# Two-layer encoder trunk on one core: both ends of the program without GpSimd, and one of four low parts of the grouped heads on GpSimd

## The chip, the cores and the metric

The kernel runs on one core of one Trainium2 chip. The time is device time in microseconds (us) of one launch; the median of the runs counts. A core has TensorE (PE in the rows: matrix products and transposes, results into the accumulation memory PSUM), VectorE (DVE), ScalarE (ACT), GpSimd (POOL) and SyncE (SP, which issues the DMAs). They run side by side and wait for each other through semaphores.

## The reference, cut to what matters

Sixteen learned tokens are put ahead of 1024 tokens of width 1024. Two layers follow, each a mixer and a squared-ReLU MLP, and a last norm:

```
h = concat(meta, x)                                   # 1040 x 1024
for i in (0, 1):
    hn = rmsnorm(h, norm_attn[i])
    h = h + (even_mixer(hn) if i == 0 else odd_mixer(hn))
    h = h + relu(rmsnorm(h, norm_mlp[i]) @ w_up[i])**2 @ w_down[i]
return rmsnorm(h, norm_final)[:, 16:]
```

`even_mixer` projects once and feeds two kinds of heads: four differential heads (A), `softmax(q0 k0 + bias) - lam * softmax(q1 k1 + bias)`, and eight query heads in two groups that share keys and values (B, the grouped heads): rms-normed and rotated queries and keys, `softmax(q k) @ v`. `odd_mixer` is windowed attention. `rmsnorm(x, g) = x * rsqrt(mean(x*x) + eps) * g`.

## The kernel before

Everything lies transposed: features on the 128 partitions, the 1040 tokens along a row, in chunks of 348, 346 and 346. For precision each operand of a product is split in a high part `h` (a rounding copy) and a low part `l = x - h`, and a product is three matmuls: high by high, high by low, low by high (`mm3`, line 149). A program orders each engine's instructions ahead of time: among what its model takes to be ready it prefers what stands earlier in the code, and it gives a tile a buffer when one of its tag is free. On the chip each engine then runs its list strictly in that order.

**Opening** (lines 236 to 263). For each chunk and each of eight feature blocks k a DMA brings `hin`; the high part `hg0h` is made on VectorE for k in `HI_DVE` = 0, 2, 5 (line 245) and on ScalarE otherwise (line 247); the low part `hg0l` is made on VectorE (line 248). In the same pass the squares for the first norm are summed in two accumulators: GpSimd squares and adds blocks 0 to 2 (`SQ_POOL` = 3, lines 255 and 259), ScalarE squares the other five (line 257), VectorE adds them (line 259) and joins the two sums (line 260). `make_r` turns the sum into the row factor R: column sums on TensorE (`colsum`, line 192), an inverse root in some 13 tiny VectorE instructions (`rsqrt_small`, lines 157 to 163), a broadcast over the partitions on TensorE (`bcast_cols`, line 215) and a ScalarE copy out of PSUM (line 224). The first two projections (`early`, blocks 16 and 12) don't need R before they are evacuated.

**Grouped heads** (`attend_b`, line 691, 34 calls: 16 pairs of query tiles for each of two groups, and one call for the 16 tokens each). A call makes scores for two 128-row tiles (line 524), evacuates them with a running minimum on VectorE (line 529), takes exponentials on ScalarE (line 538) and scales by the inverse sum on GpSimd (line 700). Its second half, `pv` (line 545), comes three calls later (`AHEAD` = 3): the probabilities are transposed on TensorE in four runs of 512 columns (line 558); each run is copied to a high part `ph` on ScalarE (line 575), its low part `plo` is formed on VectorE (line 577), and TensorE multiplies both with the values (line 589). A last short piece (lines 599 to 602) handles 16 tokens. `pv` has a way for chosen runs (`lo_pool`): transposed first, copied raw on ScalarE, both parts formed on GpSimd in buffers of their own (`ph2`, `plo2`, one each), multiplied last. `LO_A` and `LO_B` are empty, so it isn't used. Probabilities of the A and B heads share one tag, `sp`, with `A_SP` = 11 buffers.

**End** (`dense(1, ...)`, last loop). The last products of the second MLP run for three groups of tokens (512, 256 and 256, `CH_LAST`). For each of eight blocks m: products (line 149), VectorE adds them to `hall` (line 1088), `finish1` squares on ScalarE (line 183), adds into `accf` (line 184; GpSimd in the first two groups, VectorE in the last) and scales by the gain on ScalarE (line 1313). Then `done1` makes the row factor in `accf` (through `make_r`) and multiplies the eight blocks with it (line 1318), on GpSimd in the first two groups; in the last, blocks 1 and 4 on GpSimd (`R_POOL`) and six on VectorE. Two blocks at a time go out by DMA (line 1322).

Of the kernel before, what the change touches and what calls it, by code (L numbers as in the profile page):

```python
# [12 lines left out]
F32 = mybir.dt.float32  # L13
F32R = mybir.dt.float32r
I32 = mybir.dt.int32
AF = mybir.ActivationFunctionType
ALU = mybir.AluOpType
# [4 lines left out]
P = 128  # L22
L = 1040
NM = 16
S = 1024
KT = 8
# [4 lines left out]
CH_ALL = ((0, 348), (348, 346), (694, 346))  # L31
# [12 lines left out]
OUT_K = 2  # L44
# [7 lines left out]
B_TAIL = 0, 0  # L52
CUT_K = ()
U3 = 1
R_DVE, R_POOL = (), (1, 4)
FAST0 = (0, 1)
POOL_K = 4
LO_A = ()
LO_B = ()
PH2 = 1  # L60
SQ_POOL = 3
HI_DVE = (0, 2, 5)
AHEAD = 3
A_SP = 11
AHEAD_C = 2
C_S, C_PH = 5, 3

# [1 line left out]
def f32(ap):  # L69
    return ap.bitcast(F32)  # L70


def trunk(tc, hT, gT, w_in0, w_out0, w_up, w_down, w_in1, w_out1, rel, sinks, lamv, subln, qkn,
          onehot, ident_d, cos_d, sin_d, out, dbg=None, stop=None):
    nc = tc.nc
    V, A, G, T, D = nc.vector, nc.scalar, nc.gpsimd, nc.tensor, nc.sync
# [3 lines left out]
    def nm(s):  # L80
        uid[0] += 1
        return f"{s}_{uid[0]}"

    def pool(name, side="left", bufs=1, **kw):
        return tc.alloc_tile_pool(name=name, bufs=bufs, side=side, reuse_waits="tile", **kw)

    def lay_out(pl, tags):

        kept = {}
        for tag, shape, dt, bufs in tags:  # L90
            kept[tag] = [pl.tile(shape, dt, tag=tag, bufs=bufs, name=nm(tag))]

        def get(tag, shape, dt, bufs):
            if kept.get(tag):
                return kept[tag].pop()
            return pl.tile(shape, dt, tag=tag, bufs=bufs, name=nm(tag))

        return get
# [4 lines left out]
    sm = pool("small", bufs=16)  # L103
    tp = pool("temps", bufs=3)
# [3 lines left out]
    def bank(ring):  # L108
        i = at.get(ring, 0)
        at[ring] = i + 1  # L110
        tag = RINGS[ring][i % len(RINGS[ring])]
        return psU.tile([P, 512], F32, tag=tag, bufs=BANKS[tag], name=nm(ring))
# [6 lines left out]
    gt = cst.tile([P, 5, KT], F32, name="gt")  # L119
# [50 lines left out]
    def tok_tiles(c0, n):  # L170
        return [(c0 + i * P, min(P, n - i * P)) for i in range((n + P - 1) // P)]
# [6 lines left out]
    def sq_acc(hk, acc, first, o, n, add_on=G):  # L178
        if first:
            A.activation(acc[:, o:o + n], hk[:, o:o + n], AF.Square)  # L180
        else:
            t = sqp[0].tile([P, 512], F32, tag="sq", bufs=1, name=nm("sq"))
            A.activation(t[:, :n], hk[:, o:o + n], AF.Square)
            add_on.tensor_tensor(acc[:, o:o + n], acc[:, o:o + n], t[:, :n], op=ALU.add)

    def colsum(acc, c0, n, ps, scale, eps=None, on=V):

        tiles = tok_tiles(c0, n)
        accs = acc if isinstance(acc, list) else [acc]
        for i, (o, w) in enumerate(tiles):  # L190
            for j, a in enumerate(accs):
                T.matmul(ps[:w, 2 * i:2 * i + 2], a[:, o:o + w], ones, start=(j == 0), stop=(j == len(accs) - 1))
        x = sm.tile([P, 24], F32, tag="cs", bufs=2, name=nm("cs"))
        nt = len(tiles)
        full = sum(1 for _, w in tiles if w == P)
        src = ps.rearrange("p (a b) -> p a b", b=2)
        if full < nt:
            V.memset(x[:, :nt], 1.0)
        if eps is None:
            V.tensor_scalar(x[:, :full], src[:, :full, 0], scale, EPS, op0=ALU.mult, op1=ALU.add)  # L200
        else:
            V.scalar_tensor_tensor(x[:, :full], src[:, :full, 0], scale, eps, op0=ALU.mult, op1=ALU.add)
        if full < nt:
            w = tiles[-1][1]
            V.tensor_scalar(x[:w, full:nt], src[:w, full:nt, 0], scale, EPS, op0=ALU.mult, op1=ALU.add)
        return rsqrt_small(x[:, :nt], P, nt, on), tiles

    def bcast_cols(y, tiles, newps, use):

        for b in range(0, len(tiles), 4):  # L210
            ps = newps()
            off = 0
            for i in range(b, min(b + 4, len(tiles))):
                w = tiles[i][1]
                T.matmul(ps[:, off:off + w], y[:w, i:i + 1].to_broadcast([w, P]), ident[:w, :w],  # L215
                         start=True, stop=True)
                off += w
            use(ps, tiles[b][0], off)

    def make_r(acc, c0, n, smps, newps):  # L220

        y, tiles = colsum(acc, c0, n, smps, 1.0 / 1024)
        r = acc
        bcast_cols(y, tiles, newps, lambda ps, o, w: A.copy(r[:, o:o + w], ps[:, :w]))
        return r
# [6 lines left out]
    getP = lay_out(pP, [("hl", [P, L], F32R, 4), ("zT", [P, L], F32, 2), ("vst", [P, NT, P], F32R, 2)])  # L232
    xh = [xp0.tile([P, L], F32R, tag="xh", name=f"hg0h{k}") for k in range(KT)]
    xl = [xp0.tile([P, L], F32R, tag="xl", name=f"hg0l{k}") for k in range(KT)]
    hin = [pR.tile([P, L], F32, tag="hin", bufs=8, name=f"hin{k}") for k in range(KT)]
    first_w = load_w(w_in0[16], parts=2)
    D.dma_start(gt, gT)
    sq0 = cst.tile([P, L], F32, tag="ra", name="sq0")
    sq = [sq0, f32(getP("hl", [P, L], F32R, 4))]
    for o, n in CH_ALL:  # L240
        c = slice(o, o + n)
        for k in range(KT):
            D.dma_start(hin[k][:, c], hT[k][:, c])
            if k in HI_DVE:
                V.tensor_scalar(xh[k][:, c], hin[k][:, c], gt[:, 0, k:k + 1], None, op0=ALU.mult)
            else:
                A.activation(xh[k][:, c], hin[k][:, c], AF.Copy, bias=0.0, scale=gt[:, 0, k:k + 1])
            V.scalar_tensor_tensor(xl[k][:, c], hin[k][:, c], gt[:, 0, k:k + 1], f32(xh[k][:, c]),
                                   op0=ALU.mult, op1=ALU.subtract)
            on_pool = k < SQ_POOL  # L250
            acc = sq[0] if on_pool else sq[1]
            first = k in (0, SQ_POOL)
            t = acc[:, c] if first else tp.tile([P, 520], F32, tag="t", name=nm("sq"))[:, :n]
            if on_pool:
                G.tensor_tensor(t, hin[k][:, c], hin[k][:, c], op=ALU.mult)
            else:
                A.activation(t, hin[k][:, c], AF.Square)
            if not first:
                (G if on_pool else V).tensor_tensor(acc[:, c], acc[:, c], t, op=ALU.add)
        V.tensor_tensor(sq0[:, c], sq0[:, c], sq[1][:, c], op=ALU.add)  # L260
    D.dma_start(ident, ident_d)
    R = make_r(sq0, 0, L, bank("nat"), lambda: bank("nat"))

# [157 lines left out]
    n = 260  # L421
    for o in range(0, 2080, n):
        ps = bank("nat")
        T.matmul(ps[:4, :n], relt[:, 0:4], oh[o // L][:, o % L:o % L + n], start=True, stop=True)
        t = tp.tile([P, 520], F32, tag="t", name=nm("bv"))[:, :512]
# [29 lines left out]
    for h in range(4):  # L455
# [9 lines left out]
        def put_tail(pt, b, n, w):  # L465
# [12 lines left out]
    pA = pool("att", side="left")  # L478
    getA = lay_out(pA, [("sp", [P, L], F32, A_SP), ("osq", [P, L], F32, 1), ("ph", [P, 512], F32R, 3),
                        ("plo", [P, 512], F32R, 3), ("oT", [P, L], F32, 2), ("ob", [64, 256], F32, 2),  # L480
# [123 lines left out]
    def prob():  # L604
        return getA("sp", [P, L], F32, A_SP)

# [84 lines left out]
    def attend_b(g, ptq, store):  # L691
# [10 lines left out]
        def values():  # L702
            po = bank("pv")
            yield from pv(po, ptiles, (vp[g],), ((0, 0), (0, 1)), LO_B)
            gw = sum(c for _, c, _ in ptiles)
# [33 lines left out]
    if stop == "mix0":  # L739
        tt = pool("dbgp", side="right", bufs=2)  # L740
        for k in range(8):
            m = tt.tile([P, L], F32, tag="m", name=nm("m"))
# [355 lines left out]
    ht = [hp0.tile([P, L], F32, tag="h", name=nm("h")) for _ in range(KT)]  # L1098
# [98 lines left out]
    for b in range(0, 10, 4):  # L1197
        n = min(4, 10 - b)
        pt = bank("tr")
        for i in range(n):  # L1200
            o = 16 + (b + i) * P
# [13 lines left out]
    for j in range(8):  # L1215
# [10 lines left out]
        w = load_w(w_in1[j], G)  # L1226
        for t in range(8):
# [17 lines left out]
            for e in range(2):  # L1245
                ps = bank("sc1")
# [58 lines left out]
    hall = hp1.tile([P, KT, L], F32, tag="h", bufs=1, name="hall")  # L1305
    ht = [hall[:, k, :] for k in range(KT)]
    accf = []

    def finish1(m, o, n):
        if not accf:  # L1310
            accf.append(cst.tile([P, L], F32, tag="ra", name="accf"))
        sq_acc(ht[m], accf[0], m == 0, o, n, V if o + n == L else G)
        A.activation(ht[m][:, o:o + n], ht[m][:, o:o + n], AF.Copy, bias=0.0, scale=gt[:, 4, m:m + 1])

    def done1(o, n):
        make_r(accf[0], o, n, bank("sm"), lambda: bank("sm"))
        for k in range(KT):
            (G if o + n < L and k not in R_DVE or k in R_POOL else V).tensor_tensor(ht[k][:, o:o + n], ht[k][:, o:o + n], accf[0][:, o:o + n],
                                                       op=ALU.mult)
            if k % OUT_K == OUT_K - 1:  # L1320
                ks = slice(k + 1 - OUT_K, k + 1)
                D.dma_start(out[ks, :, o - 16:o - 16 + n].rearrange("k p t -> p k t"), hall[:, ks, o:o + n])

    dense(1, CH_REAL, (16, 528), 512, w_out1, hd, xp1, yp, st1, ht, POOL_K, 7, finish1, done1, [[c] for c in CH_LAST],
          lambda: [[big(yp, t, 8)[:, :512] for t in "hl"] for _ in range(2)])
# [79 lines left out]
```

## Time and profile before

| | |
|---|---|
| median of 3 runs | 2539.95 us (2537.41 to 2542.29) |
| the profiled execution, its own time | 2548.52 us |
| its span, first to last instruction | 2546.6 us |
| TensorE, VectorE, GpSimd, ScalarE busy | 96%, 74%, 50%, 50% of the span |
| mean granted TensorE clock | 0.977 of full speed |

The busy share is a mean over stages with different limits, so the rows below are read by stage: what an engine did in a stretch, what ended its waits, and how long single instructions took. A name in a row is the tile written, then "<-" and the tiles read. Matmuls overlap, so their pace is the distance from one start to the next, not the duration.

### The profile page before, as it was taken

The page shows a single profiled execution, that of the slowest core. Times are in us where ns is not written, and L with a number is a line of the kernel's source. Part 1 is how long each engine was busy: PE and PEld are TensorE (multiplying, and loading weights), DVE is VectorE, ACT ScalarE, POOL GpSimd, SP SyncE. Part 2 cuts the span into 40 slices and gives each one's busy share as a digit, 9 for nine tenths or more (in the row PEclk, how much of TensorE's full clock was granted, in tenths as well). Part 3 has the DMA queues.
Part 4 walks back from the last instruction along what each step waited for, and adds up shares of the span by engine and source line. Part 5 has one row for each costly group of instructions (what it writes and reads, how often), then busy time and mean ns, then how long its engine had stood idle before and what let it go on. Part 6 is the DMA issues. An engine that isn't in the chain of part 4 may idle for free. (4 is left out here: it accounts for less than half of the span.)

```text
span 2546.6 us, 42961 instructions
## 1 busy us (share of the span) xinstructions
PE 2441.2 (96%) x15375; PEld 2223.3 (87%) x15375; DVE 1878.6 (74%) x4035; ACT 1261.2 (50%) x2523; POOL 1280.8 (50%) x1245
## 2 busy tenths in 40 slices
PE   7999999999998999989999999998989999999997
PEld 7989888899998999989999988887868888777786
DVE  7843987799757666679898857787585555889875
ACT  3321776688634334453433547887344444443424
POOL 3300776333155555546555345556466563566645
PEclk9999999899998999999999999999999999999998
DMA  4288534000231643353433342231313443554411
GB/s 135 92 261 261 149 106 125 15 13 11 86 110 64 203 157 141 126 210 110 167 110 109 123 121 74 68 108 45 124 60 139 145 155 131 197 159 134 148 62 71
DMA packets 134614, 307.16 MB, mean 121 GB/s; under 512 B 18656, under 2 KB 49792, under 8 KB 133888
## 3 DMA queue, kind: packets, MB, share of 16 engines
q1 hardware_dynamic: 134400, 304.42, 36.6%
q8 instruction: 121, 1.98, 0.3%
q14 instruction: 93, 0.76, 0.1%
HBM read 214.43 MB, written 98.43 MB: 123 GB/s over the span
## 5 line engine op out<-in xcount | busy, mean ns | idle before, releaser
L882 PE MATMUL st<-h,wh 128*128 128x260 f32 (+1 forms) x2520 | 807.7, 325 | 27.2 <-ACT wh L132 8.4
L882 PE MATMUL st<-l,wh 128*128 128x260 f32 (+1 forms) x2520 | 809.8, 324 | 8.6 <-DVE l L807 4.1
L882 PE MATMUL st<-h,wl 128*128 128x260 f32 (+1 forms) x2520 | 780.3, 324 | 4.5 <-POOL wl L133 2.4
L882 PEld LDWEIGHTS st<-h,wh 128*128 128x128 f32 x2520 | 479.1, 191 | 74.1 <-ACT wh L132 12.4
L882 PEld LDWEIGHTS st<-l,wh 128*128 128x128 f32 x2520 | 481.2, 191 | 48.2 <-DVE l L1015 5.2
L882 PEld LDWEIGHTS st<-h,wl 128*128 128x128 f32 x2520 | 473.6, 191 | 47.3 <-POOL wl L133 6.7
L132 ACT CAST wh<-wr 128x512 fp32r<-128x512 f32 x378 | 233.1, 619 | 457.9 <-PE st L882 221.8
L133 DVE TENSOR_TENSOR wl<-wr,wh 128x512 fp32r<-128x512 f32 x254 | 230.1, 908 | 171.8 <-ACT wh L132 163.6
L133 POOL TENSOR_TENSOR wl<-wr,wh 128x512 fp32r<-128x512 f32 x124 | 173.3, 1398 | 151.4 <-ACT wh L132 141.1
L524 PE MATMUL sc<-stk,stk 128*128 128x346 f32 (+1 forms) x768 | 179.1, 351 | 4.0 <-DVE mx L526 3.3
L1046 DVE TENSOR_TENSOR h<-h,st 128x260 f32<-128x260 f32 x392 | 151.1, 418 | 28.4 <-PE st L882 27.3
L538 ACT ACTIVATE sp<-sp,mn 128x1040 f32<-128x1040 f32 x134 | 156.5, 1168 | 30.2 <-DVE mn L536 23.5
L1015 DVE TENSOR_TENSOR l<-l,h 128x520 fp32r<-128x520 f32 (+1 forms) x182 | 168.2, 926 | 1.7 <-ACT h L1013 1.7
L892 POOL TENSOR_TENSOR ws<-wr 128x512 f32<-128x512 f32 x32 | 43.9, 1373 | 216.3 <-DMA wr<-w_up 187.9
L1046 DVE TENSOR_TENSOR hall<-hall,st 128x512 f32<-128x512 f32 x196 | 131.4, 681 | 27.9 <-PE st L882 26.4
L149 PE MATMUL mm<-l,wh 128*128 128x346 f32 (+3 forms) x440 | 151.1, 343 | 0.3 <-DVE l L790 0.2
L132 ACT CAST wh<-ws 128x512 fp32r<-128x512 f32 x120 | 74.5, 621 | 155.1 <-PE st L882 118.5
L149 PE MATMUL mm<-h,wl 128*128 128x346 f32 (+3 forms) x440 | 150.0, 343 | 0.0
L149 PE MATMUL mm<-h,wh 128*128 128x346 f32 (+3 forms) x440 | 148.5, 343 | 0.9 <-ACT h L789 0.9
L577 DVE TENSOR_TENSOR plo<-tr,ph 128x512 fp32r<-128x512 f32 (+1 forms) x212 | 136.0, 646 | 17.9 <-ACT ph L575 16.6
L133 DVE TENSOR_TENSOR wl<-ws,wh 128x512 fp32r<-128x512 f32 x120 | 118.1, 984 | 38.9 <-ACT wh L132 37.8
L700 POOL TENSOR_SCALAR sp<-sp,rsum 128x1040 f32<-128x1040 f32 x66 | 75.2, 1151 | 141.8 <-DVE rsum L542 61.7
(292 smaller groups left out, 5872.4 us busy)
## 6 DMA issues: line engine op xcount, KB each, us to landing
wr<-w_down SPq DMA_DIRECT2D x68, 512.0 KB, 4.1
wr<-w_up SPq DMA_DIRECT2D x64, 512.0 KB, 4.8
l<-sd SPq DMA_DIRECT2D x42, 520.0 KB, 5.3
l<-sd SPq DMA_DIRECT2D x42, 512.0 KB, 5.3
stk<-stk_d SPq DMA_DIRECT2D x72, 260.0 KB, 7.4
sd<-up SPq DMA_DIRECT2D x30, 520.0 KB, 2.6
sd<-up SPq DMA_DIRECT2D x30, 512.0 KB, 3.0
wr<-w_in SPq DMA_DIRECT2D x27, 512.0 KB, 6.4
```

Source lines behind the costliest of these rows:

```text
L132: A.copy(h, src)
L133: lo_on.tensor_tensor(l, src, f32(h), op=ALU.subtract)
L149: T.matmul(ps[:, :n], a[:, k % 4 * P:(k % 4 + 1) * P], x[k][:, o:o + n], start=(k == 0 and i == 0), stop=(k == len(xh) - 1 and i == 2))
L524: T.matmul(ps[:M, :n], q, k[:, o:o + n], start=(i == 0), stop=(i == len(ops) - 1))
L538: A.activation(s[:M, :L], s[:M, :L], AF.Exp, bias=mn[:M, x:x + 1], scale=-1.0, accum_out=sums[:M, x:x + 1])
L577: V.tensor_tensor(plo[:, :w], pt[:, :w], f32(ph[:, :w]), op=ALU.subtract)
L700: G.tensor_scalar(s, s, rs[:, i:i + 1], 1.0, op0=ALU.mult, op1=ALU.mult)
L882: T.matmul(acc_[x, o][:, :n], a[:, c], b[:, o:o + n], start=first and k == 0 and y == 0, stop=k == nk - 1 and y == 2, skip_group_check=not ...
L892: G.tensor_tensor(s1, a21, a22, op=ALU.add)
L1015: V.tensor_tensor(l, src, f32(h), op=ALU.subtract)
L1046: marks.append(V.tensor_tensor(ht[m][:, c], ht[m][:, c], acc_[x, o][:, :n], op=ALU.add).ins)
```

## The change

In the opening all high parts go to ScalarE, and the squares move to a second loop behind the first: ScalarE squares all eight blocks, VectorE adds them into one accumulator, GpSimd does nothing. At the end `finish1` adds on VectorE in all groups; `done1` no longer copies the broadcast factor out of PSUM but multiplies all eight blocks on VectorE straight from PSUM. In the grouped heads run 0 of each `pv` takes the `lo_pool` way. `A_SP` goes from 11 to 10.

```diff
-R_DVE, R_POOL = (), (1, 4)
-LO_B = ()
+LO_B = (0,)
-SQ_POOL = 3
-HI_DVE = (0, 2, 5)
-A_SP = 11
+A_SP = 10
...
             D.dma_start(hin[k][:, c], hT[k][:, c])
-            if k in HI_DVE:
-                V.tensor_scalar(xh[k][:, c], hin[k][:, c], gt[:, 0, k:k + 1], None, op0=ALU.mult)
-            else:
-                A.activation(xh[k][:, c], hin[k][:, c], AF.Copy, bias=0.0, scale=gt[:, 0, k:k + 1])
+            A.activation(xh[k][:, c], hin[k][:, c], AF.Copy, bias=0.0, scale=gt[:, 0, k:k + 1])
...
-            if on_pool:
-                G.tensor_tensor(t, hin[k][:, c], hin[k][:, c], op=ALU.mult)
-            else:
-                A.activation(t, hin[k][:, c], AF.Square)
-            if not first:
-                (G if on_pool else V).tensor_tensor(acc[:, c], acc[:, c], t, op=ALU.add)
-        V.tensor_tensor(sq0[:, c], sq0[:, c], sq[1][:, c], op=ALU.add)
+    for o, n in CH_ALL:
+        c = slice(o, o + n)
+        A.activation(sq0[:, c], hin[0][:, c], AF.Square)
+        for k in range(1, KT):
+            t = tp.tile([P, 520], F32, tag="t", name=nm("sq"))[:, :n]
+            A.activation(t, hin[k][:, c], AF.Square)
+            V.tensor_tensor(sq0[:, c], sq0[:, c], t, op=ALU.add)
...
-        sq_acc(ht[m], accf[0], m == 0, o, n, V if o + n == L else G)
+        sq_acc(ht[m], accf[0], m == 0, o, n, V)
...
-        make_r(accf[0], o, n, bank("sm"), lambda: bank("sm"))
-        for k in range(KT):
-            (G if o + n < L and k not in R_DVE or k in R_POOL else V).tensor_tensor(ht[k][:, o:o + n], ht[k][:, o:o + n], accf[0][:, o:o + n],
-                                                       op=ALU.mult)
...
+        y, tiles = colsum(accf[0], o, n, bank("sm"), 1.0 / 1024)
+        def scale(ps, c, w):
+            for k in range(KT):
+                V.tensor_tensor(ht[k][:, c:c + w], ht[k][:, c:c + w], ps[:, :w], op=ALU.mult)
...
+        bcast_cols(y, tiles, lambda: bank("sm"), scale)
```

## Rows read from the trace of the kernel before

**Rows 1.** Busy by stretch: us, then busy us (instructions) of each engine, clock, DMA.

```profile
core 0: us, PE busy (x) PEld busy (x) DVE busy (x) ACT busy (x) POOL busy (x), PEclk, DMA share, GB/s
5.00:34.00 29.00, 19.20 (x70) 16.38 (x71) 28.40 (x45) 13.79 (x30) 16.08 (x17) 0.82 0.63 212
150.00:200.00 50.00, 48.37 (x306) 47.26 (x306) 15.19 (x25) 9.51 (x17) 0.00 (x0) 1.00 0.99 286
497.00:650.00 153.00, 151.51 (x1159) 145.37 (x1159) 150.21 (x515) 130.46 (x246) 55.19 (x51) 1.00 0.05 12
2514.00:2525.00 11.00, 10.91 (x94) 10.71 (x92) 7.74 (x12) 4.26 (x9) 10.01 (x9) 1.00 0.31 119
2525.00:2546.60 21.60, 5.50 (x22) 4.92 (x22) 12.64 (x35) 5.15 (x12) 8.69 (x11) 0.55 0.38 135
```

**Rows 2.** Opening, waits, 5 to 34 us: total us, times, longest.

```profile
PEld proj L149 <- DVE hg0l L248: 10.5, 7, 2.1
```

**Rows 3.** Opening, instructions reading hin: ns min/median/max, first and last start (us).

```profile
L243 SPq DMA_DIRECT2D hin<-hT x24: 327/402/432, 2.1 to 13.5; - x24
L248 DVE SCALAR_TENSOR_TENSOR hg0l<-hin,gt,hg0h x24: 566/571/1742, 7.6 to 32.5; 128x346 fp32r<-128x346 f32 x16, 128x348 fp32r<-128x348 f32 x8
L247 ACT ACTIVATE hg0h<-hin,gt x15: 567/573/588, 6.1 to 23.5; 128x346 fp32r<-128x346 f32 x10, 128x348 fp32r<-128x348 f32 x5
L257 ACT ACTIVATE sq<-hin x12: 475/492/496, 8.7 to 39.4; 128x346 f32<-128x346 f32 x8, 128x348 f32<-128x348 f32 x4
L245 DVE TENSOR_SCALAR hg0h<-hin,gt x9: 386/396/1062, 5.6 to 28.4; 128x346 fp32r<-128x346 f32 x6, 128x348 fp32r<-128x348 f32 x3
DMA to landing us min/median/max: 3.8/4.0/4.2
```

**Rows 4.** Opening, TensorE in order of time: start us, duration us.

```profile
12.96 0.49 PE L149 MATMUL proj<-hg0l,wh 128*128 128x348 f32 x1
13.26 0.49 PE L149 MATMUL proj<-hg0h,wl 128*128 128x348 f32 x1
...
33.90 0.32 PE L149 MATMUL proj<-hg0h,wh 128*128 128x346 f32 x1
34.06 0.39 PE L192 MATMUL nat<-ones,sq 128*128 128x2 f32 x3
```

**Rows 5.** Grouped heads, 497 to 650 us, by line, columns as in group 3.

```profile
L577 DVE TENSOR_TENSOR plo<-tr,ph x98: 658/686/693, 497.2 to 649.1; 128x512 fp32r<-128x512 f32 x98
L575 ACT CAST ph<-tr x98: 562/587/598, 497.7 to 649.0; 128x512 fp32r<-128x512 f32 x98
L700 POOL TENSOR_SCALAR sp<-sp,rsum x51: 1128/1136/1157, 495.9 to 650.0; 128x1040 f32<-128x1040 f32 x51
```

**Rows 6.** Grouped heads, waits, 497 to 650 us.

```profile
PEld pv L589 <- DVE plo L577: 5.2, 15, 0.4
```

**Rows 7.** Second MLP's opening, GpSimd making high and low parts, columns as above.

```profile
L786 POOL TENSOR_SCALAR h<-l x8: 605/622/1584, 1714.2 to 1725.4; 128x520 fp32r<-128x520 f32 x4, 128x504 fp32r<-128x504 f32 x4
L787 POOL TENSOR_TENSOR l<-l,h x8: 1250/1282/1737, 1715.4 to 1731.5; 128x520 fp32r<-128x520 f32 x4, 128x504 fp32r<-128x504 f32 x4
```

**Rows 8.** A heads, waits of TensorE, 300 to 470 us.

```profile
PE pv L589 <- ACT ph L575: 4.8, 3, 2.4
```

**Rows 9.** End, GpSimd in order of time: start, duration, count, idle before.

```profile
2515.72 10.47 POOL L1318 TENSOR_TENSOR hall<-hall,accf 128x512 f32<-128x512 f32 x8 [0.53 <-ACT accf L224]
```

**Rows 10.** End, VectorE in order of time.

```profile
2508.59 0.17 DVE L157 TENSOR_SCALAR rst<-cs 128x4 int32<-128x4 int32 x1
...
2518.50 1.26 DVE L157 TENSOR_SCALAR rst<-cs 128x2 int32<-128x2 int32 x1
...
2531.43 0.42 DVE L1088 TENSOR_TENSOR hall<-hall,mm 128x256 f32<-128x256 f32 x1 [0.20 <-PE mm L149]
...
2534.16 0.61 DVE L157 TENSOR_SCALAR rst<-cs 128x2 int32<-128x2 int32 x1
...
2539.96 3.15 DVE L1318 TENSOR_TENSOR hall<-hall,accf 128x256 f32<-128x256 f32 x6 [1.78 <-ACT accf L224]
```

**Rows 11.** End, TensorE in order of time.

```profile
2524.64 0.28 PE L149 MATMUL mm<-l,h 128*128 128x256 f32 x1
2528.06 1.19 PE L215 MATMUL sm<-ident,rsy 128*128 128x128 f32 x4 [3.15 <-DVE rsy L163]
```

More of the change, by code (lines that the diff above doesn't have):

```diff
@@ L238, in trunk @@
     sq0 = cst.tile([P, L], F32, tag="ra", name="sq0")
-    sq = [sq0, f32(getP("hl", [P, L], F32R, 4))]
     for o, n in CH_ALL:
@@ L243, in trunk @@
             D.dma_start(hin[k][:, c], hT[k][:, c])
-            if k in HI_DVE:
-                V.tensor_scalar(xh[k][:, c], hin[k][:, c], gt[:, 0, k:k + 1], None, op0=ALU.mult)
-            else:
-                A.activation(xh[k][:, c], hin[k][:, c], AF.Copy, bias=0.0, scale=gt[:, 0, k:k + 1])
+            A.activation(xh[k][:, c], hin[k][:, c], AF.Copy, bias=0.0, scale=gt[:, 0, k:k + 1])
             V.scalar_tensor_tensor(xl[k][:, c], hin[k][:, c], gt[:, 0, k:k + 1], f32(xh[k][:, c]),
                                    op0=ALU.mult, op1=ALU.subtract)
[L250 to L253, printed above, removed]
-            if on_pool:
-                G.tensor_tensor(t, hin[k][:, c], hin[k][:, c], op=ALU.mult)
-            else:
-                A.activation(t, hin[k][:, c], AF.Square)
-            if not first:
-                (G if on_pool else V).tensor_tensor(acc[:, c], acc[:, c], t, op=ALU.add)
-        V.tensor_tensor(sq0[:, c], sq0[:, c], sq[1][:, c], op=ALU.add)
+    for o, n in CH_ALL:
[5 more added lines that the diff above has]
+            V.tensor_tensor(sq0[:, c], sq0[:, c], t, op=ALU.add)
     D.dma_start(ident, ident_d)
@@ L1311, in finish1 @@
             accf.append(cst.tile([P, L], F32, tag="ra", name="accf"))
-        sq_acc(ht[m], accf[0], m == 0, o, n, V if o + n == L else G)
+        sq_acc(ht[m], accf[0], m == 0, o, n, V)
         A.activation(ht[m][:, o:o + n], ht[m][:, o:o + n], AF.Copy, bias=0.0, scale=gt[:, 4, m:m + 1])
     def done1(o, n):
-        make_r(accf[0], o, n, bank("sm"), lambda: bank("sm"))
-        for k in range(KT):
-            (G if o + n < L and k not in R_DVE or k in R_POOL else V).tensor_tensor(ht[k][:, o:o + n], ht[k][:, o:o + n], accf[0][:, o:o + n],
-                                                       op=ALU.mult)
-            if k % OUT_K == OUT_K - 1:
-                ks = slice(k + 1 - OUT_K, k + 1)
-                D.dma_start(out[ks, :, o - 16:o - 16 + n].rearrange("k p t -> p k t"), hall[:, ks, o:o + n])
+        y, tiles = colsum(accf[0], o, n, bank("sm"), 1.0 / 1024)
+        def scale(ps, c, w):
+            for k in range(KT):
+                V.tensor_tensor(ht[k][:, c:c + w], ht[k][:, c:c + w], ps[:, :w], op=ALU.mult)
+                if k % OUT_K == OUT_K - 1:
+                    ks = slice(k + 1 - OUT_K, k + 1)
+                    D.dma_start(out[ks, :, c - 16:c - 16 + w].rearrange("k p t -> p k t"), hall[:, ks, c:c + w])
+        bcast_cols(y, tiles, lambda: bank("sm"), scale)
     dense(1, CH_REAL, (16, 528), 512, w_out1, hd, xp1, yp, st1, ht, POOL_K, 7, finish1, done1, [[c] for c in CH_LAST],
```

## The prediction

> **What bounds the kernel now.** I read the busy shares by stretch first, then the waits of each stretch that the change touches, then single instructions. TensorE has the most work over the whole span, and between the ends it seldom stands still, so the change can pay only where TensorE is held up by another engine, or behind its last product. There are three such places.
>
> In the opening VectorE is the bound: from 5 to 34 us it is busy 28.40 of 29 us, while TensorE gets through only 70 matmuls [rows 1]. TensorE's weight loads wait 10.5 us for `hg0l`, the low part that VectorE makes at line 248 [rows 2]. The data is there much earlier: the last `hin` is issued at 13.5 us and lands some 4.0 us later, but the last `hg0l` starts at 32.5 us [rows 3].
>
> In the grouped heads, TensorE (151.5 of 153 us) and VectorE (150.2) are both full, ScalarE is at 130.5, and GpSimd has two thirds of its time free [rows 1]. Matmul ends are modelled, so the TensorE figure alone doesn't say that nothing can be won. The waits say that it is held up a little: its loads wait 5.2 us, 15 times, for the low part `plo` of line 577 [rows 6].
>
> At the end GpSimd multiplies eight blocks in one piece, 10.47 us from 2515.72 [rows 9]. Meanwhile the tiny VectorE instructions of the next group's inverse root stretch: line 157 takes 1.26 us where it took 0.17 before GpSimd began [rows 10]. So the root is late, and TensorE, whose next instruction in order is the broadcast of it, stands for 3.15 us to 2528.06 [rows 11]. Behind that the clock is low, 0.55 on average from 2525 on [rows 1]. In the last group line 157 is slow again, 0.61 us [rows 10].
>
> **Opening.** Off VectorE go nine high parts of 0.396 us (3.6 us at the median, more with the stretched ones: 1.062 at most) and the stretching of line 248, whose median is 0.571 and whose worst is 1.742 us [rows 3], while GpSimd is busy for 16 us beside it [rows 1]. On ScalarE stand 24 high parts of 0.573 (13.8 us), then 24 squares of 0.492 (11.8 us) [rows 3]; it was busy for 13.8 of 29 us [rows 1], and the squares now come after all high parts in the code. On VectorE stand 24 low parts (13.7 us), then 21 adds; for an add I take the 0.57 us of line 248, which has the same shape: 12 us. When is the last low part done? Not before the data: 13.5 + 4.0 + 0.57 + 0.57 = 18.6 us. Not after all adds have gone ahead of it: 7.6 + 13.7 + 12 = 33.3, no gain at all. The adds stand behind the low parts in the code, so I take 22 us, 11 earlier than now.
>
> How much of that does TensorE see? Its 70 matmuls cost 0.16 us each at full clock (33.90 to 34.06) and 0.30 at half (12.96 to 13.26) [rows 4]. It starts at about 6.7 us in either kernel. The first 24 at half clock and 46 at full make 7.2 + 7.4 = 14.6 us, so it is where it now is at 34.06 by 21.3 us if nothing holds it and by some 25 us if the last low parts pace it. I take 8 us, bounds 0 and 11. What is late next is R: the adds end at about 7.6 + 13.7 + 12 + 2 (weights' low parts) = 35 us, and TensorE by then has the second early projection, which doesn't need R, and a third whose evacuation does. R's last sum now comes at over 40 us, so R moves forward as much as TensorE does. **Opening: -8 us.**
>
> **End.** The 3.15 us stand goes. Twelve matmuls and the broadcast that follow it at half clock (to 2531.4, 3.4 us [rows 10, 11]) run at full: some 1.7 us less. So TensorE ends about 4.8 us earlier. Then the last chain: the root's first four instructions lose the 0.45 us each that they take over 0.17 [rows 10], 1.8 us. The ScalarE copy of the factor goes: VectorE waited 1.78 us for broadcast and copy together [rows 10]; I put the copy at 0.4. The multiplications become eight on VectorE instead of six in 3.15 us beside two on GpSimd [rows 10]; at line 1088's 0.42 us, also from PSUM, eight take 3.4 at most, so between +0.2 and -0.5: nothing. Together 4.8 + 1.8 + 0.4 = 7.0. Against it: VectorE takes over 14 adds and 16 multiplications. In the stretch of the third group (2514 to 2525) it is busy for 7.74 of 11 us, part of that stretched [rows 1]; what comes in is about eight multiplications of 256 columns and the rest of those of 512 (0.69 us by line 577's row of that size [rows 5]), 5 to 6 us, against the 4 to 5 us of stretching that leave. So the last adds may queue for up to a microsecond; if these terms all come at their worst the gain halves. **End: -6.5 us, bounds -3 and -8.5.**
>
> The Trainium skill has a rule for this contention, "SBUF — State Buffer", section "Who interferes with whom": VectorE and GpSimd share one pair of ports, held by whoever started first for the whole instruction, and a VectorE instruction with at most one SBUF input outside the two-port modes doesn't contend. By it the new multiplications, which take one factor from PSUM, would be free of it even beside GpSimd, and the end term stays; by contention as in the stretched rows, it would stay too, since GpSimd has nothing left there.
>
> **Grouped heads.** One of four low parts leaves VectorE: 0.686 us per call [rows 5]. 98 of them in 153 us are 24.5 calls, 6.24 us each. VectorE would have 10% less, so up to 34 x 0.69 = 23 us if it alone were the bound; nothing if TensorE is really full. The nearest row for what TensorE loses is its wait for `plo`, 5.2 us in 24.5 calls [rows 6], 7.2 us in 34. ScalarE keeps its load: the raw copy takes the place of the rounding copy (0.587 [rows 5]). GpSimd gets 0.62 + 1.28 us per call [rows 7] beside two scalings of 1.136 [rows 5]: 4.2 of 6.24 us, so it keeps up on average. I take **-6 us, bounds 0 and -13** (the wait row, and about twice that, as other VectorE delays shrink with it). That the new GpSimd work stretches VectorE as at the end is not seen here: line 577 stays within 658 to 693 ns through the whole stretch though GpSimd is busy for 55 us of it [rows 1, 5].
>
> The Trainium skill speaks against this part: "GPSIMD Engine Reference", section 4.1 "Engine selection", tells to put elementwise work with two inputs on VectorE, since GpSimd is about twice as slow. The rows here agree on the durations (1.28 against 0.69 us). By the rule alone the move loses 0.6 us per call; by the rows it moves work from a full engine to one with room, and counts only if GpSimd's result comes late, which is the third rival.
>
> **A_SP from 11 to 10.** Three waiting A groups hold 2 + 2 + 3 probability tiles and the one in work up to 4: eleven. With ten the fourth has to wait for one to come free. No row shows a wait for such a tile. The nearest row is the wait of TensorE for the softmax side in the A heads, 4.8 us in 3 times, 2.4 at most [rows 8]; one more of its mean length in each of four heads is 6.4. Below zero it may go by a reordering, 1 us. **+2 us, bounds -1 and +6.**
>
> **Sum.** -8 - 6.5 - 6 + 2 = -18.5 us on the profiled execution's 2548.5, so 2530.0. That execution took 8.6 us more than the median of the runs; on the median the forecast is 2521.5, with a range of its own of 2510 to 2532.
>
> **Rivals.** First, TensorE is really full in the grouped heads, and freeing VectorE there gives nothing: -12.5, 2527.5. For it speaks the 151.5 of 153 us; against it the waits for `plo`. Second, the opening's gain is given back: from 150 to 200 us the DMA engines are busy for 0.99 of the time [rows 1], and an earlier TensorE may only wait for its data there. If the grouped heads give nothing either, what is left is -6.5 + 2 = -4.5: 2535.5, no change by the measure that 0.2% (5 us) is about what can be told from none. Against it: those transfers are themselves started by results that come earlier. Third, on the other side: GpSimd's part of run 0 ends late. Its chain is 0.59 + 0.62 + 1.28 and some 0.3 of hand-overs, 2.8 us, and if two scalings stand ahead of it in GpSimd's order 5.1. Its cover is the rest of the call's TensorE work: 6.24 less the run's own transposes and products (a quarter of two thirds, 1.1) and the tail, 4.5 us. From 4.5 on every microsecond counts 34 times, because TensorE's order is fixed and the single `ph2` lets no second run start early: 0.6 us late is +20, with the ends and A_SP together +8: 2548. For it speaks that GpSimd now waits long in this stretch for others; against it that the scalings belong to a call three ahead.
>
> **How the numbers follow.** The forecast 0.55; the first rival 0.16; the second 0.14; the third 0.15. Faster 0.71, same 0.14, slower 0.15. The range takes in the first and second rivals and the lower bounds of the terms, and stops short of the third: 2508 to 2545.
>
> **What would show it.** Right: the last `hg0l` near 22 us, TensorE's seventieth matmul near 25, no stretched line 248; the grouped heads' calls at about 6.05 us with no wait of TensorE for `plo2`; no stand of TensorE before its last broadcast and line 157 at 0.17 us in all groups. Wrong: adds of the squares ahead of low parts on VectorE; TensorE standing before the products of run 0; new waits of a microsecond or more in the A heads.

## The result, and the profile after

The changed kernel takes 2566.49 us (median of 4 runs, 2559.71 to 2567.88) where the kernel before takes 2540.42 beside it (4 runs). The ratio is 1.0095, interval 1.0077 to 1.0112: 1% slower. The profiled execution of after took 2567.69 us, its span is 2565.7. That of before lay 8 us above its median, so the two spans differ by 19.1 us only. In what follows a stage is compared by spans, a whole kernel by medians.

First where the stages lie. Three lines of after give it: the first score (line 514), the copy at the end of each grouped call (line 697), the products of the two MLPs (line 872). Columns as in [rows 3].

```profile
L514 PEld LDWEIGHTS sc<-stk,stk x768: 186/189/338, 248.2 to 675.1; 128*128 128x128 f32 x192
L697 ACT COPY ob<-pv x34: 263/370/372, 473.7 to 716.0; 64x256 f32<-64x256 f32 x32, 64x128 f32<-64x128 f32 x2
L872 PEld LDWEIGHTS st<-h,wh x2520: 186/188/338, 799.4 to 2507.5; 128*128 128x128 f32 x194
```

The same three lines of every kernel, from its own trace (us; "heads" is from the first call's copy to the first MLP product, so it holds all grouped calls but the first, and what stands behind them):

| kernel | first score | A heads, to the first copy | heads | MLP products | behind them | span |
|---|---|---|---|---|---|---|
| before | 257.9 | 224.8 | 294.4 | 1706.7 | 62.8 | 2546.6 |
| after | 248.2 | 225.5 | 325.7 | 1708.1 | 58.2 | 2565.7 |
| new ends alone | 247.3 | 221.7 | 294.3 | 1703.9 | 58.3 | 2525.5 |
| ends, ten buffers | 248.2 | 228.3 | 293.0 | 1704.3 | 58.7 | 2532.5 |
| all, split later | 247.8 | 228.1 | 300.2 | 1707.9 | 59.1 | 2543.1 |
| ten buffers alone | 258.0 | 233.6 | 295.8 | 1707.6 | 62.8 | 2557.8 |
| middle alone | 256.5 | 235.7 | 326.4 | 1707.0 | 63.1 | 2588.7 |

The opening gave 9.7 us, the end 4.6, and the grouped heads took 31.3. Busy by stretch in after, columns as in [rows 1]:

```profile
5.00:34.00 29.00, 24.75 (x123) 21.09 (x124) 26.65 (x57) 23.26 (x52) 4.67 (x5) 1.00 0.75 242
150.00:200.00 50.00, 50.00 (x319) 49.92 (x318) 18.15 (x30) 10.98 (x18) 0.00 (x0) 1.00 1.00 314
497.00:650.00 153.00, 141.90 (x1005) 125.92 (x1004) 123.32 (x427) 110.10 (x213) 89.92 (x87) 1.00 0.04 10
```

In the opening TensorE gets through 123 matmuls instead of 70. From 150 to 200 us it never stands, though the DMA engines are full: the gain isn't given back there. In the grouped heads the three engines that were near full do less: TensorE 1005 matmuls instead of 1159, VectorE 123 us instead of 150, ScalarE 110 instead of 130. No engine is full, so this stretch is bound by waits. They are, from 493 to 670 us (columns as in [rows 2]):

```profile
POOL ph L560 <- PE pv L579: 47.1, 20, 4.1
ACT praw L558 <- PE tr L548: 43.8, 22, 2.3
PEld pv L579 <- ACT ph L565: 16.8, 21, 0.8
DVE plo L567 <- ACT ph L565: 14.6, 24, 1.1
PE pv L579 <- ACT ph L565: 11.8, 20, 0.6
PEld pv L579 <- DVE plo L567: 7.9, 25, 0.5
```

No line has TensorE waiting for GpSimd. GpSimd's own subtraction, asked for by line, has nobody behind it in these 177 us (nothing follows its last line), and line 560, which makes `ph` on GpSimd, has none either:

```profile
L562 POOL TENSOR_TENSOR plo<-praw,ph x25: 1274/1285/1308, 494.7 to 663.6; 128x512 fp32r<-128x512 f32 x25
...
who waited for it (us, times):
```

What is new is that ScalarE stands before the raw copy (line 558), 43.8 us in 22 calls, 2.0 us each, waiting for TensorE's transposes, while TensorE waits for ScalarE's copies `ph`. One turn of that circle in order of time, the accumulator reads left out:

```profile
537.38 1.08 ACT L565 CAST ph<-tr 128x512 fp32r<-128x512 f32 x2
...
538.02 0.39 PE L579 MATMUL pv<-ph,v 128*128 128x256 f32 x1 [0.60 <-ACT ph L565]
...
538.48 0.37 ACT L591 CAST tail<-tr 32x256 fp32r<-32x256 f32 x1
...
538.81 1.28 DVE L567 TENSOR_TENSOR plo<-tr,ph 128x512 fp32r<-128x512 f32 x2
539.55 0.38 PE L579 MATMUL pv<-plo,v 128*128 128x256 f32 x1
...
540.13 0.60 PE L548 MATMUL tr<-ident,sp 128*128 128x128 f32 x4
...
540.82 0.59 ACT L558 COPY praw<-tr 128x512 f32<-128x512 f32 x1 [1.97 <-PE tr L548]
...
541.30 1.17 ACT L528 ACTIVATE sp<-sp,mn 128x1040 f32<-128x1040 f32 x1
...
542.46 0.58 ACT L565 CAST ph<-tr 128x512 fp32r<-128x512 f32 x1
...
542.92 1.18 ACT L528 ACTIVATE sp<-sp,mn 128x1040 f32<-128x1040 f32 x1
...
544.61 1.08 ACT L565 CAST ph<-tr 128x512 fp32r<-128x512 f32 x2
```

ScalarE copies the last two `ph` of a call (537.38). VectorE forms their low parts (538.81). TensorE multiplies with them (539.55), and only behind four of these products stand, in its order, the transposes of the next call's run 0 (540.13). For those ScalarE has been standing since its `tail` copy ended at 538.85, because the raw copy is next in its own order. Both exponentials and the three `ph` copies of the next call queue behind it, and TensorE waits 0.58 us for the first of the last pair, to 545.24. From the one pair of copies to the next it is 7.23 us, against 6.24 before.

### The profile page after: what moved, and what is told of

It is laid out like the page before. It is cut to its first block, busy times and chain, and to the rows that moved or that the text cites. A ratio compares the mean times of both kernels' runs of the same rounds, so it can differ in the third digit from the quotient of the medians.

```text
span 2565.7 us, 42903 instructions
## 1 busy us (share of the span) xinstructions
PE 2446.4 (95%) x15375; PEld 2209.7 (86%) x15375; DVE 1860.4 (73%) x4030; ACT 1264.1 (49%) x2538; POOL 1298.0 (51%) x1266
## 5 line engine op out<-in xcount | busy, mean ns | idle before, releaser
L579 PE MATMUL pv<-ph,v 128*128 128x256 f32 (+2 forms) x528 | 132.9, 293 | 19.0 <-ACT ph L565 18.9
L908 ACT ACTIVATE up<-up 128x520 f32<-128x520 f32 (+1 forms) x128 | 81.1, 636 | 132.9 <-DVE up L905 132.6
```

The costliest lines, as they stand in the source:

```text
L579: T.matmul(ps_o[:, :gw], vmats[v][:, j, :], (plo if lo else ph)[:, c], start=n_ == 0, stop=False)
L908: A.activation(r[:, c], r[:, c], AF.Square)
```

## The experiments

The question was which part costs, and then what in the grouped heads: GpSimd late, the single pair `ph2`, `plo2`, the order of the copies, or the ten buffers. Ratios are to the kernel before, run on the same chip.

**The ends alone, the middle alone.** The first is the changed kernel with:

```diff
-LO_B = (0,)
+LO_B = ()
-A_SP = 10
+A_SP = 11
```

> The changed kernel with LO_B empty and A_SP 11: only the opening and the end differ from the kernel before. In the changed kernel the first scores start 9.7 us earlier than before, and the stretch from the last large MLP product to the end of the span is 4.6 us shorter. Theory 1 (the loss sits in the grouped heads alone): some 14 us faster than before, 2526. Rival (the opening's gain is given back later whatever the heads do): 5 us faster at most, 2535.

Measured: 2528.22 us beside 2543.91, ratio 0.9945 (0.9926 to 0.9964), 15.7 us faster. The second is the kernel before with the opposite two lines.

> The kernel before with LO_B = (0,) and A_SP = 10: the middle of the change alone. Theory 1 (the loss sits in the grouped heads): a call takes 7.1 to 7.2 us instead of 6.2, the stretch of the 34 calls is about 28 us longer, 2568 to 2578 in all. Rival (the earlier opening made another order in the heads, and the new low parts are harmless): 2535 to 2545.

Measured: 2592.87, ratio 1.0200 (1.0171 to 1.0228), with the same heads as after: 326.4 us against 294.4. It is 15 us above the range expected, which had counted the grouped heads alone; the A heads are 10.9 us longer too. So the ends are as good as forecast, and everything lost is in the middle.

**Run 0 without GpSimd.** Middle alone, `PH2` = 2, but both parts straight from PSUM on ScalarE and VectorE, still in the order of `lo_pool`:

```diff
-                raw = tp.tile([P, 520], F32, tag="t", name=nm("praw"))[:, :512]
-                A.copy(raw[:, :w], pt[:, :w])
...
-                G.tensor_scalar(ph[:, :w], raw[:, :w], 1.0, 1.0, op0=ALU.mult, op1=ALU.mult)
+                A.copy(ph[:, :w], pt[:, :w])
...
-                G.tensor_tensor(plo[:, :w], raw[:, :w], f32(ph[:, :w]), op=ALU.subtract)
+                V.tensor_tensor(plo[:, :w], pt[:, :w], f32(ph[:, :w]), op=ALU.subtract)
```

> The middle alone, but run 0 of the grouped heads is only transposed first and multiplied last: its high part is made on ScalarE and its low part on VectorE straight from PSUM, in two pairs of buffers, as for the other runs. Theory A (the loss is the order: the early transposes and what stands behind the copy of them on ScalarE): a call stays at 7 us or more, about 2565. Theory B (the loss is GpSimd's chain and its hand-overs): back to 6.2 to 6.4 us a call, 2540 to 2545.

Measured: 2570.82, ratio 1.0112 (1.0079 to 1.0145); heads 309.2 us. Neither theory fits: the calls are short, as B said (6.4 us), the total is A's. ScalarE stands for 0.4 us in 12 copies of run 0. What differs is TensorE's order:

```profile
541.94 0.60 PE L558 MATMUL tr<-ident,sp 128*128 128x128 f32 x4
...
542.74 0.59 ACT L568 CAST ph<-tr 128x512 fp32r<-128x512 f32 x1
...
543.58 0.39 PE L587 MATMUL pv<-plo,v 128*128 128x256 f32 x1
```

Run 0 of the next call is transposed at 541.94, ahead of the last call's products that need VectorE, not behind them. Taking a run ahead is not what costs by itself; the two engines' orders must fit. From the first call's copy to the last it is 205.3 us, less than the 212.2 with ten buffers alone (below); the heads' loss lies behind the last call. There the next stage begins, with 576 products of line 149 (`mm`): the kernel before, after and the ten buffers alone have over 80 of them among the last calls, this kernel has none, and from the last copy to the first MLP product it is 103.9 us instead of 83.6, with TensorE waiting there 6.2 us for ScalarE's `h` (line 787), 0.9 in the kernel before. Why the program placed them so isn't shown.

**Two pairs of buffers.** Middle alone with `PH2` = 2.

> The middle alone with two pairs ph2 and plo2 instead of one. GpSimd waits 47 us in the heads for the products that free the single pair. Theory C (the single pair ties each call to the one before): a call falls to 6.0 to 6.4 us, 2530 to 2545. Theory A (ScalarE's order): no change from the middle alone, about 2570.

Measured: 2599.94, ratio 1.0227 (1.0193 to 1.0260). From 520 to 700 us of it:

```profile
POOL ph L570 <- ACT praw L568: 51.2, 24, 4.1
ACT praw L568 <- PE tr L558: 45.6, 23, 2.2
```

GpSimd no longer waits for products to free its one pair, yet ScalarE stands for 2.0 us a call as before, and with one pair or two the calls take 6.3 and 8.4 us in turn. The single pair isn't the cause. The 7 us above the middle alone go with the products of the next stage: here too none stands among the last calls, and behind the last copy it is 104.3 us against 83.5.

**Ten buffers alone.** The kernel before with `A_SP` = 10.

> The kernel before with A_SP = 10 and nothing else. The middle alone made the A heads (first scores to the last tail product) 10.8 us longer than before, 235.2 against 224.4, and the last step into the grouped heads 3.4 us. Theory (the tenth and not the new low parts does that): the A heads again at 235, the grouped heads at 6.2 us a call, 2550 to 2556 in all. Rival (the eleventh buffer was idle, the low parts changed the order in the A heads too): 2538 to 2543. A third: ten buffers already slow the grouped heads, a call at 6.8 or more, 2565.

Measured: 2559.17, ratio 1.0063 (1.0046 to 1.0080), 16.9 us slower, 3 above the range expected, with the same number of instructions on every engine, in another order. The A heads take 233.6 us instead of 224.8. Waits from 258 to 490 us, first of before, then with ten buffers:

```profile
PEld sc L524 <- DVE mx L526: 9.0, 24, 2.0
PE sc L524 <- DVE mx L526: 3.3, 3, 1.8
DVE sp L526 <- POOL sp L647: 0.2, 1, 0.2
DVE beta L645 <- ACT sp L538: 3.3, 4, 1.4
```

```profile
PEld sc L524 <- DVE mx L526: 17.5, 29, 3.6
PE sc L524 <- DVE mx L526: 10.3, 7, 3.3
DVE sp L526 <- POOL sp L648: 4.9, 4, 2.0
DVE beta L645 <- ACT sp L538: 13.9, 9, 6.0
```

VectorE evacuates scores into a new `sp` (line 526), and now has to wait four times until GpSimd has read the old one (line 648). TensorE's next scores then wait for VectorE to empty the bank. That direct wait is 4.9 us only. VectorE also waits 13.9 us instead of 3.3 before line 645 for ScalarE's exponentials: with another number of buffers the program ordered the lists otherwise, and the runs don't separate the missing buffer from the new order.

**The raw copy one run later.** Middle alone; run 0 is transposed and copied raw behind the first of the other runs:

```diff
-        slow = {r: split(r) for r in lo_pool}
-        order = [r for r in range(len(runs)) if r not in slow] + list(lo_pool)
+        slow = {}
+        order = [r for r in range(len(runs)) if r not in lo_pool] + list(lo_pool)
...
             ph, plo = slow[r] if r in slow else split(r)
+            if r == order[0]:
+                slow = {x: split(x) for x in lo_pool}
```

> The middle alone, but run 0 is transposed and copied raw behind the split of the first normal run, not ahead of it; GpSimd still forms its parts and its products still come last. Theory A (ScalarE's raw copy stands ahead of exponentials and waits 2 us a call for transposes that TensorE comes to late, and TensorE then waits for what stands behind it on ScalarE): the wait of the raw copy shrinks and a call falls to 6.2 to 6.6 us, 2550 to 2565. Theory B (the GpSimd way as such, wherever it starts): 7.1 us a call, about 2590.

Measured: 2561.44, ratio 1.0074 (1.0054 to 1.0094). Heads 297.5 us, against 326.4 with the same work split first and 295.8 with ten buffers and no GpSimd run. Some thirty of the fifty microseconds that the middle alone loses hang on the place of run 0's transposes and copy.

**The opening alone, the end alone.** The kernel before with the new opening, and with the new end; the rest of the change undone.

> The kernel before with the opening of the changed one. By the prediction's term 8 us faster, by the trace of the changed kernel, whose first scores start 9.7 us earlier, 10: 2530 to 2533. Rival: given back in the A heads, 2537 to 2543.

> The kernel before with the end of the changed one. By the prediction's term 6.5 us faster, by the traces, where the stretch from the last large MLP product to the end of the span is 4.5 us shorter, 2535 to 2537. Rival: VectorE's longer queue gives it all back, 2540 to 2543.

Measured: opening 2532.52, ratio 0.9962 (0.9947 to 0.9976), 9.8 us faster; end 2538.59, ratio 0.9987 (0.9978 to 0.9997), 3.7 us faster, 1.6 us short of the range expected. Both beside 2542.31.

**The parts put together.** New ends with ten buffers and no GpSimd run (`LO_B` = ()); the whole change with the later split; the same with eleven buffers, the room taken from `ph` and `plo` (two buffers each, not three); new ends with twelve buffers.

> The changed kernel with its new opening and end and ten probability buffers, but no run of low parts on GpSimd. Theory: the loss has two parts, ten buffers in the A heads and the order of ScalarE in the grouped heads. Without the second the calls take 6.2 us again; ten buffers cost between 4 us (the A stage of the changed kernel is 225.1 us, that of the ends alone 221.3) and 17 us (measured with the old opening), so 2532 to 2545. Rival: the loss is all in the grouped heads' order, ten buffers cost something only beside the old opening: 2528, as the ends alone.

> The whole change, with GpSimd's run transposed and copied raw after the first of the other runs instead of ahead of them. Theory (ScalarE's raw copy stands ahead of its turn and closes a circle of waits): calls at 6.1 to 6.2 us instead of 7.1, 20 to 25 us come back, 2540 to 2546, within 3 us of the same kernel without the run on GpSimd. Rival (GpSimd's run costs as such, and the old opening hid it): above 2555, calls near 7.

> As the whole change with the later split, but eleven probability buffers; the room comes from the high and low parts of the other runs, two buffers each instead of three. Theory: the two costs are gone and GpSimd's help is left, some 0.1 us per call: 2525, at or a little below the ends alone (2528). Rival: two buffers of parts are too few for the A heads, which have no run on GpSimd: TensorE waits there for the copies, 2535 to 2545.

> The new ends, no run on GpSimd, twelve probability buffers. If the A heads are short of buffers step by step, a twelfth takes some of VectorE's and TensorE's waits there away: 3 to 8 us below the ends alone, 2520 to 2525, A stage below 220 us. If eleven are what three waiting groups and the one in work hold at most, nothing: 2528, A stage 221.

Measured, all beside 2542.09:

| kernel | us | ratio, interval |
|---|---|---|
| ends, ten buffers | 2533.76 | 0.9965 (0.9952 to 0.9978) |
| all, split later | 2542.81 | 1.0002 (0.9993 to 1.0012) |
| all, split later, eleven buffers | 2531.60 | 0.9954 (0.9935 to 0.9972) |
| ends, twelve buffers | 2530.63 | 0.9953 (0.9937 to 0.9969) |

The later split inside the whole change brings the loss from 26.1 us down to 0.7. From 513 to 585 us, first after, then the later split: ScalarE's groups (line, busy us and mean ns, idle before and its cause) and the stretch.

```profile
L558 ACT COPY praw<-tr 128x512 f32<-128x512 f32 x10 | 5.9, 588 | 20.8 <-PE tr L548 20.8
...
513.00:585.00 72.00, 65.58 (x456) 57.08 (x455) 57.34 (x195) 50.47 (x100) 40.79 (x40) 1.00 0.05 10
```

```profile
L528 ACT ACTIVATE sp<-sp,mn 128x1040 f32<-128x1040 f32 x25 | 29.2, 1169 | 9.5 <-DVE mn L526 9.5
...
L558 ACT COPY praw<-tr 128x512 f32<-128x512 f32 x12 | 6.8, 569 | 0.0
...
513.00:585.00 72.00, 71.69 (x549) 68.50 (x548) 66.39 (x234) 62.20 (x119) 48.39 (x47) 1.00 0.05 12
```

The stand before the raw copy is gone, and TensorE is back at 549 matmuls and 71.69 of 72 us. VectorE has 5.6 us of room, ScalarE 9.8, GpSimd does its 48. And yet a call is hardly shorter than without the GpSimd run: six calls in a row take 36.7 us, with ten buffers and no GpSimd run 37.2. At the first calls, at the turn from the first group to the second and at the last calls it loses some 8 us again, so its heads take 300.2 us against 293.0, and the kernel is 9 us above the same one without the run, not within 3. Why these places suffer wasn't followed up. So far as the runs go, the low part on GpSimd never paid: without it the ends make 2528.22, and neither eleven buffers beside a later split nor twelve buffers get below that, though the intervals overlap. Neither expectation for the eleven came true: two buffers of parts don't lengthen the A heads (221.6 us, the ends alone 221.7), but the heads take 298.4. Twelve shorten the A heads to 217.4 us and the way from the first call's copy to the last to 197.4 (the ends alone 210.4); but here too the next stage's products stand all behind the last call, which shortens the one and makes the other 106.0 us instead of 83.9, and the heads take 303.4. So what a twelfth buffer is worth with those products in their old place isn't known. The ends alone have the lowest time of this study.

## Why the prediction was wrong, step by step

The forecast was 18.5 us faster, the runs show 26.1 slower: 44.6 apart. By differences of medians, each to the kernel before of its own call:

| step | forecast | measured | from |
|---|---|---|---|
| opening and end | -14.5 | -15.7 | ends alone |
| `A_SP` 11 to 10 | +2 | +7.4 | ends with ten buffers less ends alone |
| grouped heads | -6 | +34.4 | after less ends with ten buffers |

**Grouped heads: the step that failed.** The term was made from VectorE's load and from TensorE's wait for `plo`, and GpSimd's side was bounded by its work, 4.2 of 6.24 us. All that held: the low part left VectorE, GpSimd kept up, line 562 took 1.285 us against the 1.28 assumed, and VectorE was not stretched (line 567 has 686 ns at the median, 671 to 694). What was missing is ScalarE. The text said it "keeps its load", and it does; but the copy that it keeps was moved to another place in its fixed order, ahead of both exponentials, and it depends on transposes that TensorE makes behind products waiting for ScalarE's own last copies. Its load was never the limit: 50.47 us busy in the 72 us above, some 5.1 a call, and 2.1 a call standing at the raw copy, which make 7.2 of a call's 7.3. Of the 34.4 us the later split gives back 25.4; the other 9.0 stay with it, and their cause is open. The sum counted an operation that moves at the difference of its durations, 0; it should have asked what stands behind it on its engine, and when its input is there. The range of 0 to -13 had no bound above nothing.

**The third rival** named the right stage and the right side, at 0.15, by a wrong mechanism. It had GpSimd's chain too late for its products, from 4.5 us on. No product waited for it. The single `ph2` did hold GpSimd back, 47.1 us, as its sentence said, but that cost nothing: with two pairs the calls kept their length. The second rival (opening given back) is refuted by the opening alone, 9.8 us faster, and by TensorE's 50.00 of 50 us. The first (TensorE full, nothing gained in the heads) named a time that didn't come, but its premise is not refuted: in the later split, where the stand is gone, TensorE is busy 71.69 of 72 us and a call is under 0.1 us shorter than without the run, some 3 us in 34 calls where the forecast had 6.

The Trainium skill's rule on engine choice ("GPSIMD Engine Reference", section 4.1) warned against this part, and the part lost. But the runs don't show the loss where the rule puts it: GpSimd was as slow as the page says, 1.285 against 0.686 us, and nobody waited.

**`A_SP`: wrong size, the mechanism only in part.** The fourth group does wait for a tile to come free, but VectorE's direct wait for it is 4.9 us with the old opening and 2.3 with the new (ends with ten buffers, 3 times), where the price is 16.9 and 7.4. The bound was taken from TensorE's wait for copies, 6.4 at most. With the old opening another wait grew: TensorE's scores for VectorE, from 12.3 to 27.8 us in the A heads, whose loads and products partly overlap. With the new one it did not, 16.1 us in the ends alone and 13.4 with ten buffers. The A heads of these two, first the ends alone, then with ten buffers, columns as in [rows 1]:

```profile
247.30:469.00 221.70, 208.96 (x1430) 192.60 (x1429) 190.73 (x767) 159.12 (x316) 145.32 (x141) 0.96 0.41 110
```

```profile
248.20:476.50 228.30, 214.43 (x1430) 195.99 (x1428) 189.67 (x760) 158.33 (x315) 145.34 (x141) 0.94 0.40 107
```

TensorE stands 1.1 us longer with ten buffers (13.9 against 12.7), but is busy 5.5 us longer with the same number of matmuls, at a mean granted clock of 0.94 instead of 0.96. So most of the 6.6 us here shows as slower matmuls at the lower clock, not as waits; why the price depends on the opening is open. With the old opening the traces have 8.8 us in the A heads.

**Opening: right in size, by another order.** It gave 9.8 us alone, 9.7 by the first score, for 8. By instruction:

```profile
L240 ACT ACTIVATE hg0h<-hin,gt x24: 567/570/585, 5.4 to 21.6; 128x346 fp32r<-128x346 f32 x16, 128x348 fp32r<-128x348 f32 x8
L241 DVE SCALAR_TENSOR_TENSOR hg0l<-hin,gt,hg0h x24: 578/582/1739, 6.0 to 24.3; 128x346 fp32r<-128x346 f32 x16, 128x348 fp32r<-128x348 f32 x8
...
PEld proj L146 <- DVE hg0l L241: 4.8, 10, 1.6
```

The last low part starts at 24.3 us instead of 32.5 (forecast: done near 22), and TensorE is past its seventieth matmul by 25 us, as said. But ten of the 21 adds, 5.2 us, stand ahead of the last low part on VectorE, which the forecast had named as a sign of being wrong: the sum had all adds behind. That the gain came out all the same is partly luck. The 0.30 us per matmul that the forecast called half clock stands at a granted clock of 1.00 (12 to 14 us, before), so the clock isn't shown as its reason; in after the pace goes from 0.29 to 0.16 us at 12 us, also at 1.00. The worst low part still takes 1.739 us, so "no stretched line" was wrong; GpSimd is still busy for 4.67 us of this stretch, but whether that is the cause isn't shown.

**End: right in every piece but one.** VectorE and TensorE of after, in order of time:

```profile
2549.53 0.28 PE L146 MATMUL mm<-h,l 128*128 128x256 f32 x1
2552.70 0.68 PE L212 MATMUL sm<-ident,rsy 128*128 128x128 f32 x4 [2.90 <-DVE rsy L160]
2553.22 0.51 PE L189 MATMUL sm<-ones,accf 128*128 128x2 f32 x4
```

```profile
2552.06 0.43 DVE L181 TENSOR_TENSOR accf<-accf,sq 128x256 f32<-128x256 f32 x1
...
2553.42 2.74 DVE L1311 TENSOR_TENSOR hall<-hall,sm 128x256 f32<-128x256 f32 x8 [0.87 <-PE sm L212]
2556.08 0.15 DVE L197 TENSOR_SCALAR cs<-sm 128x2 f32<-128x2 f32 x1
2556.27 0.17 DVE L154 TENSOR_SCALAR rst<-cs 128x2 int32<-128x2 int32 x1
...
2558.24 0.16 DVE L160 SCALAR_TENSOR_TENSOR rsy<-rst,rsy 128x2 f32<-128x2 f32 x1
2559.78 2.74 DVE L1311 TENSOR_TENSOR hall<-hall,sm 128x256 f32<-128x256 f32 x8 [1.38 <-PE sm L212]
```

From the last MLP product (line 872) to the last product of line 146 it is 5.1 us less than before (forecast 4.8). The last root takes 2.1 us instead of 4.0 (forecast 1.8 less), the wait for the factor 1.38 instead of 1.78 [rows 10], the eight multiplications 2.74 instead of 3.15. The term that was too small is the queue on VectorE, put at "up to a microsecond": the third group's root is woven into the last adds, and its eight multiplications (2.74 us) now stand ahead of the last column sum's reader. From the last product to the start of the last root it is 6.7 us instead of 3.2. Hence 4.6 us by the trace, 3.7 by the run, not 6.5; still within the bounds of 3 to 8.5.

The Trainium skill's rule on shared ports ("SBUF — State Buffer", "Who interferes with whom") agrees with the short instructions back at 0.16 us where GpSimd is silent, and with line 567, one operand from PSUM, unstretched beside 25 GpSimd subtractions. Whether the new multiplications would stay so short beside GpSimd no run here shows; the nearest row is line 1088 of the kernel before, of the same shape and with one operand in PSUM, 0.42 and 0.41 us at 2517.19 and 2520.92, within GpSimd's 10.47 [rows 9].

## What to carry to other kernels

When an operation is moved ahead on an engine that runs its list in order, ask first when its input is made, and by which instructions on which engine; then list all that is queued behind it. An engine that is busy for 70% of a stretch can still set its pace, if its stand lies in a circle: in the trace two engines then wait for each other, and none is full. And a buffer given up for a new path has a price of its own in the stage that shares it: measure the change of the pool alone. And when a stage's time changes, look also where the next stage's instructions were placed: in three kernels of this study shorter calls were lost again in a longer stretch behind the last one.

## What was not expected of the hardware

Eight multiplications of 256 columns with one factor in PSUM take 2.74 us on VectorE, back to back with GpSimd silent. In the kernel before six with both factors in SBUF took 3.15 [rows 10]. They differ in the place of a factor and in GpSimd beside them, and the trace of before separates the two:

```profile
2540.30 0.95 DVE L1318 TENSOR_TENSOR hall<-hall,accf 128x256 f32<-128x256 f32 x1
...
2540.01 1.82 POOL L1318 TENSOR_TENSOR hall<-hall,accf 128x256 f32<-128x256 f32 x2 [3.22 <-ACT accf L224]
```

Two of the six (this one and the next, 0.94 us at 2541.17) began while GpSimd multiplied, 2540.01 to 2541.83. The other four took 0.41 to 0.43 us, as long as those with a factor in PSUM (0.42 at the median of line 1311). So the two were stretched beside GpSimd, and the place of the factor alone made no difference. GpSimd's subtractions in the grouped heads (1274 to 1308 ns) and VectorE's (671 to 694) don't disturb each other, while the whole-block multiplication at the end of the kernel before stretched VectorE's smallest instructions sevenfold [rows 9, 10].
